# Three tiles find other homes, and the third convolution block's sums run beside its taps, with the conv norm ahead of the later heads' queries and keys

## The chip, the core and the metric

The kernel runs on one core of one Trainium2 chip. The metric is the device time of one execution in microseconds. The engines are TensorE (PE, with its weight loads as PEld), VectorE (DVE), ScalarE (ACT), GpSimd (POOL) and SyncE (SP), which here only issues DMAs.

## The reference

One layer of a hybrid decoder on x of 1024 tokens by 1024 features, all in float32:

```python
h = rms_norm(x, norm1_g)
q, k, v, glu_a, glu_b = split(h @ w_in)          # 5 x 512 columns
A = stick_breaking_attention(norm(q), norm(k), v) # 8 heads x 64, strictly causal
C = swish(layer_norm(causal_depthwise_conv(glu_a * sigmoid(glu_b))))  # width 31, 512 channels
x = x + concat([A, C]) @ w_out
h = rms_norm(x, norm2_g)
g, v = split(h @ w_up)                            # 2 x 2816
x = x + (silu(causal_dwconv3(g)) * v) @ w_down
```

Stick-breaking attention weighs a key by the sigmoid of its score and by the product of one minus the sigmoids of all later keys; the kernel does this with logs, a running sum and an exponential. The layer norm of the convolution is over the 512 channels of a token.

## The kernel before, in words

**Products.** Each float32 operand is split into a high part, rounded to what TensorE takes (`hi`), and a remainder (`lo`). A product is three matmuls: high by high, low by high, high by low (`mm3`, L280 to L283). Products of the queries, keys and values of heads 0 to 3 are 256 columns wide, others up to 512.

**Stages.** The times are those of the profiled execution.
- 0 to 35: the first norm. For each of 8 blocks of 128 tokens (`norm_in`, L383): squares on ScalarE, the root on GpSimd (L273), scaling on VectorE (L393), 8 transposes on TensorE (L402), high part on ScalarE (L406), remainder on VectorE (L407). Value products of heads 0 to 3 stand among the transposes.
- to 134: value and gate products. The convolution works on 4 blocks of 128 channels, numbered 0 to 3 here. It is split into even and odd tokens: the even taps and odd taps on VectorE with their sums in PSUM (`conv_a`, L573 and L575; `conv_b`, L583 and L585), and a third chain on sums of neighbouring inputs (`xs`, made at L559): ScalarE multiplies (L599), GpSimd adds (L602). Three closing sums on VectorE join them (L615, L616, L617; L615 needs the whole third chain).
- 134 to 181: keys and queries of heads 0 to 3. Each result bank is squared by ScalarE (L483), GpSimd takes the root (L272, L273), and ScalarE scales it out of PSUM (L487). Only then is the bank free.
- 181 to 205: values of heads 4 to 7 (copied out at L472).
- 205 to 250: queries and keys of heads 4 to 7 (`qk`) and, among them, the convolution's norm: transposes L638 (`ln`), statistics L642 and L643, scaling L646, transposes back L664 (`lnT`).
- 249 to 456: attention, head after head: keys and queries are transposed (`kT` L922, `qT` L956), scores `z` (L993 to L996), weights on ScalarE (`wt`, L1008), running sums on VectorE (L1023), products on GpSimd (L1026), transposes (`wT`, L1049), a remainder `tl` (L1059), and the output `po` (L1065, L1066). The score chain of a head leaves TensorE waiting unless other products fill it: the rest of `qk` early, and the convolution's half of the out projection (`op`) later.
- 456 to 516: attention's half of the out projection (`opa`), the second norm (L1303, L1311) and the operand blocks for the feed-forward.
- 516 to 939: the up projection, a loop over 22 blocks of features. Block products follow a Strassen-like scheme with 7 products for 8.
- 939 to the end: the down projection (`dn`, L1623). Each result bank is added to up to four sums of the output (`c11`, `c21`, `c12`, `c22`) on VectorE (L1626). The sums begin with x, loaded by DMA. The weights are split at L1531 to L1533.

**The order.** Up to the end of attention the order is not written out: each piece of work is an operation of a `Plan` with an engine, a cost, a key (`T(us)`, the wanted time, in units of 8 us), operations that it comes after, and tokens for rooms in PSUM and SBUF (`"s"` is the three banks for transposes). A list scheduler takes the ready operation that can start first; among those that start within `PATIENCE` (in ns) of an engine's being free, the smaller key wins. The order that comes out is then fixed on PE, DVE, ACT and POOL. SP's queue and all later stages are ordered by the tile scheduler. Rooms in SBUF are reused when the last reader of the old tile is done, so a tile's home decides when a load into it may begin.

Of the kernel before, what the change touches and what calls it, by code (L numbers as in the profile page):

```python
# [31 lines left out]
LEAD_LOAD, LEAD_W = 14.0, 11.0  # L32
LN_AT = 195.0
# [3 lines left out]
HORIZON, PATIENCE = 3.0, 50  # L37
AHEAD_Z, AHEAD_SCAN = 1.7, 0.9
QK_FROM, QK_TO = -3.0, 6.0
CONV_FROM, CONV_TO = 7.0, 31.0  # L40
W_SHIFT = 0.0
# [135 lines left out]
def kernel(  # L177
# [54 lines left out]
    const([P, 24], F32, "pad")  # L232

    ident = const([P, P], F32, "ident")
    make_identity(nc, ident)
    ident_b = const([P, P], BF16, "ident_b")
    nc.vector.tensor_copy(ident_b, ident)
    ident_r = const([P, P], F32R, "ident_r")
    nc.vector.tensor_copy(ident_r, ident)
# [46 lines left out]
    small = ctx.enter_context(tc.tile_pool(name="small", bufs=1))  # L286
    mix_ctx = ExitStack()
    mixp = mix_ctx.enter_context(tc.tile_pool(name="mixp", bufs=1, reuse_waits="tile"))
    attn_out = mixp.tile([P, ND // 2, S], F32, tag="attn_out", name="attn_out")
# [4 lines left out]
    for tag in ("v0", "k0", "q0", "k1", "q1", "v1"):  # L294
        tile_of = qkvp.tile([P, 2, D], F32, tag=tag, name=f"x_{tag}")
        if tag not in ("v0", "k0"):
            xs.append(tile_of)
# [3 lines left out]
    wp = in_ctx.enter_context(tc.tile_pool(name="wp", bufs=1, side="right", reuse_waits="tile"))  # L301
    hp = hp_ctx.enter_context(tc.tile_pool(name="hp", bufs=1, side="right", reuse_waits="tile"))
# [33 lines left out]
    for n in range(2):  # L336
        h_hi.append(hp.tile([P, ND, HS], F32R, tag=f"hh{n}", name=f"h_hi{n}"))
        h_lo.append(hp.tile([P, ND, HS], F32R, tag=f"hl{n}", name=f"h_lo{n}"))
# [9 lines left out]
                 "qd": 2, "squares": 1, "whl": 8, "pair": 2, "norm": 4, "xsum": 2, "cacc": 2, "term": 3, "ln": 4},  # L348
# [93 lines left out]

    def project(part, blk, ws, pairs, ats):

        done.setdefault((part, blk), [])
        for pair, at_ in zip(pairs, ats):
# [31 lines left out]
            def square(d=d, pair=pair, dst=dst, o=o):  # L478
                d["sq"], d["rs"] = [small.tile([P, 8], F32, tag=f"{tag}8_{o.index}", name=f"{tag}_{part}{blk}_{pair}") for tag in ("sq", "rs")]
                d["to"] = dst().rearrange("p t (h d) -> p (t h) d", d=DH)  # L480
                d["from"] = d["ps"].rearrange("p t (h d) -> p (t h) d", d=DH)
                for i in range(8):
                    nc.scalar.activation(d["to"][:, i, :], d["from"][:, i, :], AF.Square, accum_out=d["sq"][:, i:i + 1])  # L483

            def scale(d=d):
                for i in range(8):
                    nc.scalar.activation(d["to"][:, i, :], d["from"][:, i, :], AF.Copy, scale=d["rs"][:, i:i + 1])  # L487

            a = add("ACT", 3500, square, T(at_ + 6), [m])
            b = add("POOL", 2700, lambda d=d: rstd(d["rs"], d["sq"], 1.0 / DH), T(at_ + 6), [a])  # L490
            a = add("ACT", 1850, scale, T(at_ + 6), [b])
            o.users += [a]
            done[part, blk] += [a]
# [21 lines left out]
    def glu(c, ws, ats, conv_at, conv_to):  # L515
# [73 lines left out]
        for m in range(HALF + 1):  # L589
# [11 lines left out]
            x = add("ACT", 720, times, key(m, 16), [summed], [tm])  # L601
            last = add("POOL", 1310, lambda e=e: nc.gpsimd.tensor_tensor(d["c"], d["c"], e["t"], op=ALU.add), key(m, 16), [x, last])  # L602
# [178 lines left out]
    def queries_keys_in(t, at_):  # L781
# [3 lines left out]
        for k in range(ND):  # L785
            def products(k=k):
                if k == 0:
                    d["ps"] = bank(o, [P, 512], f"qk{t}")
                for part in "qk":
# [435 lines left out]
    for name, tag in (("11", "hh0"), ("21", "hl0"), ("22", "hh1"), ("T2", "hl1")):  # L1225
        new_block([name], hp, tag)
# [437 lines left out]
```

## Time and profile before

| | |
|---|---|
| median of 3 runs | 1165.71 us (1164.83 to 1165.88) |
| profiled execution, its own time | 1162.9 us |
| its span | 1161.1 us |
| mean granted clock of TensorE | 0.987 |
| matmuls | 5734 |

A profiled execution's span begins with its first instruction and ends with its last. In windows and groups, busy times are in us; a bracket behind a row of a timeline gives the time that the engine was idle before it and what ended that time. Since TensorE is nearly always busy, what counts is where it isn't, and where its clock is below 1.00.

### The profile page before, as it was taken

The page shows a single profiled execution, that of the slowest core. Times are in us where ns is not written, and L with a number is a line of the kernel's source. Part 1 is how long each engine was busy: PE and PEld are TensorE (multiplying, and loading weights), DVE is VectorE, ACT ScalarE, POOL GpSimd, SP SyncE. Part 2 cuts the span into 40 slices and gives each one's busy share as a digit, 9 for nine tenths or more (in the row PEclk, how much of TensorE's full clock was granted, in tenths as well). Part 3 has the DMA queues.
Part 4 walks back from the last instruction along what each step waited for, and adds up shares of the span by engine and source line. Part 5 has one row for each costly group of instructions (what it writes and reads, how often), then busy time and mean ns, then how long its engine had stood idle before and what let it go on. Part 6 is the DMA issues. An engine that isn't in the chain of part 4 may idle for free.

```text
span 1161.1 us, 16180 instructions
## 1 busy us (share of the span) xinstructions
PE 1118.5 (96%) x5734; PEld 936.9 (81%) x5734; DVE 909.5 (78%) x1199; ACT 640.3 (55%) x1335; POOL 603.2 (52%) x505
## 2 busy tenths in 40 slices
PE   6999999989999997979999999999999989999998
PEld 5888899767788886868888888888888867888886
DVE  5399995549998888889887777777677679887895
ACT  6255576586987885554434333434333466766680
POOL 6077965486666652545522332233313167877880
PEclk8999999999999998989999999999999999999999
DMA  8011103122743114432332222222222461134303
GB/s 276 19 56 55 55 2 91 47 102 95 232 126 110 55 39 153 154 127 65 118 109 71 93 73 91 73 91 73 91 86 79 133 247 70 77 145 146 130 16 145
DMA packets 108638, 116.50 MB, mean 100 GB/s; under 512 B 20782, under 2 KB 88590, under 8 KB 108558
## 3 DMA queue, kind: packets, MB, share of 16 engines
q1 hardware_dynamic: 108414, 114.95, 30.0%
q8 instruction: 45, 0.74, 0.3%
q10 hardware_dynamic: 144, 0.52, 0.1%
q14 instruction: 35, 0.29, 0.1%
HBM read 82.95 MB, written 28.31 MB: 96 GB/s over the span
## 4 chain that ended last, share of the span: by engine, by line
PE 84%; DVE 6%; POOL 4%; ACT 3%; issue 2%; DMA 1%; SPq 0%; POOLq 0%; DVEq 0%; ACTq 0%
PE dn L1623 16%; PE u_S L281 7%; PE u_S L282 7%; PE u_S L283 7%; PE u L282 5%; PE u L281 5%; PE u L283 5%; PE wT L1049 2%; POOL attn_out L602 2%; PE po L1066 2%; PE v L281 1%; PE po L1065 1%; PE v L282 1%; PE v L283 1%; PE z L996 1%
## 5 line engine op out<-in xcount | busy, mean ns | idle before, releaser
L1623 PE MATMUL dn<-wd,wd 128*128 128x512 f32 x924 | 212.4, 390 | 5.3 <-DVE c L1626 2.7
L1623 PEld LDWEIGHTS dn<-wd,wd 128*128 128x128 f32 x924 | 172.6, 188 | 44.9 <-DVE c L1626 4.8
L1626 DVE TENSOR_TENSOR c<-dn,c 128x512 f32<-128x512 f32 x144 | 95.2, 683 | 24.1 <-PE dn L1623 22.8
L602 POOL TENSOR_TENSOR attn_out<-attn_out 128x512 f32<-128x512 f32 x60 | 83.3, 1389 | 54.2 <-ACT attn_out L599 50.4
L1532 ACT CAST wd<-rawd 128x512 fp32r<-128x512 f32 x154 | 87.0, 618 | 42.1 <-PE dn L1623 15.8
L1026 POOL TENSOR_TENSOR wt<-wt,nb 128x128 f32<-128x128 f32 (+3 forms) x64 | 78.2, 1228 | 56.6 <-DVE nb L1023 34.1
L282 PE MATMUL u_S<-bT,aS 128*128 128x512 f32 x264 | 102.7, 389 | 0.0
L283 PE MATMUL u_S<-bT,aS 128*128 128x512 f32 x264 | 102.7, 389 | 0.0
L281 PE MATMUL u_S<-bT,aS 128*128 128x512 f32 x264 | 102.4, 389 | 0.0
L277 ACT CAST aS<-rawu 128x512 fp32r<-128x512 f32 x63 | 39.0, 621 | 94.8 <-PE u_S L283 70.6
L1023 DVE TENSOR_TENSOR_SCAN nb<-nb,one 128x128 f32<-128x128 f32 (+3 forms) x64 | 85.3, 1344 | 6.8 <-ACT nb L1005 6.6
L1533 DVE TENSOR_TENSOR wd<-whole,wd 128x512 fp32r<-128x512 f32 x110 | 73.7, 683 | 10.7 <-ACT wd L1532 8.4
L1392 POOL TENSOR_TENSOR s<-rawu 128x512 f32<-128x512 f32 x21 | 29.9, 1426 | 99.5 <-DMA rawu<-in_w_up_dram 89.3
L1531 ACT COPY whole<-rawd 128x512 f32<-128x512 f32 x110 | 63.0, 584 | 29.7 <-DMA rawd<-in_w_down_dram 15.7
L1398 POOL TENSOR_TENSOR rawu<-rawu 128x512 f32<-128x512 f32 x21 | 29.0, 1381 | 82.3 <-DVE a L278 82.3
L282 PE MATMUL u<-b,a 128*128 128x512 f32 x176 | 70.0, 398 | 0.0
L281 PE MATMUL u<-b,a 128*128 128x512 f32 x176 | 69.9, 397 | 0.0
L283 PE MATMUL u<-b,a 128*128 128x512 f32 x176 | 69.2, 393 | 0.0
L277 ACT CAST a<-rawu 128x512 fp32r<-128x512 f32 x63 | 39.0, 621 | 51.5 <-PE u_S L283 34.7
L1487 DVE SCALAR_TENSOR_TENSOR y<-gv,cols_a,y 128x1023 f32<-128x1023 f32 (+1 forms) x44 | 58.6, 1333 | 8.3 <-ACT y L1485 8.2
L1533 POOL TENSOR_TENSOR wd<-rawd,wd 128x512 fp32r<-128x512 f32 x44 | 57.5, 1324 | 11.6 <-ACT wd L1532 9.7
L278 DVE TENSOR_TENSOR a<-rawu,a 128x512 fp32r<-128x512 f32 x63 | 47.0, 748 | 15.8 <-ACT a L277 15.8
(286 smaller groups left out, 3363.7 us busy)
## 6 DMA issues: line engine op xcount, KB each, us to landing
rawu<-in_w_up_dram SPq DMA_DIRECT2D x44, 512.0 KB
act_d<-y SPq DMA_DIRECT2D x22, 512.0 KB
rawd<-act_d SPq DMA_DIRECT2D x22, 512.0 KB
rawd<-in_w_down_dram SPq DMA_DIRECT2D x22, 512.0 KB
rawo<-in_w_out_dram SPq DMA_DIRECT2D x8, 512.0 KB
m<-conv_d SPq DMA_DIRECT2D x16, 256.0 KB
xt<-in_x_dram SPq DMA_DIRECT2D x8, 512.0 KB
x_part<-xt SPq DMA_DIRECT2D x8, 512.0 KB
```

Of the source, the lines that this page charges most:

```text
L277: nc.scalar.copy(hi, src)
L281: nc.tensor.matmul(ps, a_hi, b_hi, start=first, stop=False)
L282: nc.tensor.matmul(ps, a_hi, b_lo, start=False, stop=False)
L283: nc.tensor.matmul(ps, a_lo, b_hi, start=False, stop=last)
L602: last = add("POOL", 1310, lambda e=e: nc.gpsimd.tensor_tensor(d["c"], d["c"], e["t"], op=ALU.add), key(m, 16), [x, last])
L1023: nc.vector.tensor_tensor_scan(rev, rev, one.to_broadcast([P, w]), 1.0, op0=ALU.mult, op1=ALU.bypass)
L1026: nc.gpsimd.tensor_tensor(d["wt"][:, :w], d["wt"][:, :w], d["nb"][:, o + 1:S + 1], op=ALU.mult)
L1531: nc.scalar.copy(whole, src)
L1532: nc.scalar.copy(t[:, 0], src)
L1533: lo_engine.tensor_tensor(t[:, 1], whole, f32(t[:, 0]), op=ALU.subtract)
L1623: nc.tensor.matmul(ps, a[:, tok], b, start=first and m == 0, stop=last and m == 2, skip_group_check=True)
L1626: nc.vector.tensor_tensor(sums[c][s], ps, sums[c][s], op=ALU.add)
```

## The change

**Three homes.**
- The identity matrix is made in a corner of `attn_out`, and only its rounded copy `ident_r` is kept and read as float32; the room of the old one goes to a small scratch tile.
- `q1` and `k1` (queries and keys of heads 4 to 7) are one tile `qk1`. Queries and keys are normalized by one function, `normalized`: the bank is first copied to SBUF whole (L452 after), and squares (L457) and scaling run from SBUF, so the bank is free after the copy. There are 12 such copies.
- The first half of the high part of h (`hh0`) has a pool of its own (`hp0`). At the end, `c11` and `c21` lie there as one tile `c_1`. Before, they lay over the operand block `T4`, which the last up product reads; now they lie over block `11`, which the first of the last seven products reads. Head 0's keys are split into a tile of the convolution (`first_keys`), and so need not wait until h is free.

**The plan's numbers.**
- The third chain's keys run over 0.6 of the window of a block (`m * 0.6`), and the windows are 29 us, not 33.
- The key of the conv norm (`LN_AT`) is 165, not 195.
- The later token blocks of the first norm are wanted at 10, 12, 14, 16 rather than 20, 23, 26, 29 us of the plan.
- Head 0's keys are wanted 4.0 units ahead of the head's own work (`EARLY`), not 2.6. `PATIENCE` goes from 50 to 200 ns. `LEAD_LOAD` (how far ahead weights are loaded), `QK_TO` (until when the `qk` filler is spread) and `W_SHIFT` (the out projection's weights) change too.

```diff
-LN_AT = 195.0
+LN_AT = 165.0
...
-        norm_in(t, xl[t], (2 + 2 * t) if t < 4 else (8 + 3 * t))
+        norm_in(t, xl[t], (2 + 2 * t) if t < 4 else (10 + 2 * (t - 4)))
...
-    ats = {0: ((24, 35), 47, 80), 1: ((58, 69), 80, 113), 2: ((80, 91), 113, 146), 3: ((102, 113), 146, 179)}
+    ats = {0: ((24, 35), 47, 76), 1: ((58, 69), 76, 105), 2: ((80, 91), 105, 134), 3: ((102, 113), 134, 163)}
...
-            x = add("ACT", 720, times, key(m, 16), [summed], [tm])
+            x = add("ACT", 720, times, key(m * 0.6, 16), [summed], [tm])
...
+    def normalized(name, d, o, m, to, at_):
+        r = plan.token("rs8")
...
+        c = add({"ACT": 600, "DVE": 690}, out_of, T(at_), [m])
+        o.users += [c]
+        a = add("ACT", 3500, square, T(at_), [c], [r])
+        b = add("POOL", 2700, lambda: rstd(d["rs"], d["sq"], 1.0 / DH), T(at_), [a])
+        a = add("ACT", 1850, scale, T(at_), [b])
...
+        k2 = split_op("k", staged, 0, base - (2.6 if h else EARLY), ready, khl)
...
+    sums = hp0.tile([P, 4, D], F32, tag="hh0", name="c_1")
...
-    sums = {c: quarters([dn.tile([P, D], F32, tag=f"c{c}_{k}", name=f"c{c}_{k}") for k in range(2)]) for c in ("11", "21")}
```

**How the order moves.** VectorE, around the second value projection, before. `lo_v` is the remainder of the value weights, `v_1898` the values copied out, `conv_b` the odd taps, and `L615` to `L617` are the closing sums of conv block 3.

```order
90 L585 SCALAR_TENSOR_TENSOR conv_b_1691<-cpad_916,cols_b,conv_b_1691 128x512 x12
91 L433 TENSOR_TENSOR lo_v_0_1810<-raw_v_0_1473,hi_v_0_1809 128x1024
92 L433 TENSOR_TENSOR lo_v_1_1827<-raw_v_1_1475,hi_v_1_1826 128x1024
93 L585 SCALAR_TENSOR_TENSOR conv_b_1691<-cpad_916,cols_b,conv_b_1691 128x512 x2
94 L472 COPY v_1898<-v_2_1899 128x512
95 L472 COPY v_1898<-v_3_1965 128x512
96 L433 TENSOR_TENSOR lo_qk_2070<-raw_qk_1851,hi_qk_2069 128x1024
97 L615 TENSOR_TENSOR attn_out<-attn_out,conv_a_1518 128x512
98 L433 TENSOR_TENSOR lo_qk_2074<-raw_qk_1867,hi_qk_2073 128x1024
99 L616 TENSOR_TENSOR conv_out_2053<-conv_a_1518,conv_out_2053 128x512
100 L617 TENSOR_TENSOR conv_out_2053<-attn_out,conv_b_1691 128x512
```

The same place after. `q_1587` are the queries of heads 0 to 3, with one copy (L452) for each pair of token blocks; L629 to L631 are the closing sums.

```order
88 L599 SCALAR_TENSOR_TENSOR conv_b_1633<-cpad_1112,cols_b,conv_b_1633 128x512 x7
89 L452 COPY q_1587<-q_1_1662 128x512
90 L599 SCALAR_TENSOR_TENSOR conv_b_1633<-cpad_1112,cols_b,conv_b_1633 128x512 x4
91 L452 COPY q_1587<-q_2_1735 128x512
92 L629 TENSOR_TENSOR attn_out<-attn_out,conv_a_1438 128x512
93 L452 COPY q_1587<-q_3_1813 128x512
94 L437 TENSOR_TENSOR lo_v_0_1891<-raw_v_0_1396,hi_v_0_1890 128x1024
95 L437 TENSOR_TENSOR lo_v_1_1895<-raw_v_1_1420,hi_v_1_1894 128x1024
96 L630 TENSOR_TENSOR conv_out_1926<-conv_a_1438,conv_out_1926 128x512
97 L631 TENSOR_TENSOR conv_out_1926<-attn_out,conv_b_1633 128x512
98 L656 BN_STATS st_0_1978<-ln_0_1968 128x6
```

The closing sums moved ahead of the values' copies, and the two value remainders moved from the middle of the taps to behind the first closing sum and the last query copy. TensorE's second matmul of this projection reads `lo_v_0`, directly behind the last query product. On GpSimd, the two remainders of the query weights (on VectorE before) and the input sum of block 2 now stand among the sums of L602 (L616 after).

TensorE, where attention begins, before: `qk` are queries and keys of heads 4 to 7, `lnT` the conv norm's transposes, `z` the scores of head 0.

```order
1378 L922 MATMUL kT_0_2599<-ident_r,keys 128x128 x4
1379 L922 MATMUL kT_1_2604<-ident_r,keys 128x128 x4
1380 L664 MATMUL lnT_2_2610<-ident,attn_out 128x128 x4
1381 L281 MATMUL qk_2561<-hi_qk_2155,h_hi_170 128x512
1382 L282 MATMUL qk_2561<-lo_qk_2156,h_hi_170 128x512
1383 L283 MATMUL qk_2561<-hi_qk_2155,h_lo_171 128x512
1384 L664 MATMUL lnT_3_2630<-ident,attn_out 128x128 x4
1385 L993 MATMUL z_0_0_2635<-keys 128x256
```

The same place after; 15 matmuls of `qk_2570` follow the transposes, and then `z_0_0` stands in row 1358.

```order
1338 L289 MATMUL qk_2515<-hi_qk_2295,h_lo_175 128x512
1339 L939 MATMUL kT_0_2540<-ident_r,first_keys 128x128 x4
1340 L939 MATMUL kT_1_2545<-ident_r,first_keys 128x128 x4
1341 L973 MATMUL qT_0_2550<-ident_r,attn_out 128x128 x4
1342 L973 MATMUL qT_1_2561<-ident_r,attn_out 128x128 x4
1343 L287 MATMUL qk_2570<-hi_qk_2073,h_hi_172 128x512
```

All of the conv norm is now ahead of this place: its transposes stand among the value products and the first `qk` products. Behind the first scores 81 matmuls of `qk` are left, and 57 before. At the end of attention, the last 68 matmuls before `opa` held no other work before; now 12 matmuls of the out projection (3, 6 and 3) stand among them.

VectorE, where the down projection begins, before: `wd` are weight remainders, `gv` and `y` belong to the last up block, `c_0` is the sum `c11`.

```order
805 L1484 TENSOR_TENSOR gv<-u_22_8508,gv 128x512
806 L1533 TENSOR_TENSOR wd_8616<-whole_8617,wd_8616 128x512
807 L1487 SCALAR_TENSOR_TENSOR y_8422<-gv,cols_a,y_8422 128x1022
808 L1533 TENSOR_TENSOR wd_8644<-whole_8645,wd_8644 128x512
809 L1626 TENSOR_TENSOR c_0_8592<-dn_2_0_8624,c_0_8592 128x512
810 L1626 TENSOR_TENSOR c_0_8592<-dn_2_1_8629,c_0_8592 128x512
```

The same place after:

```order
810 L1501 TENSOR_TENSOR gv<-u_22_8520,gv 128x512
811 L1645 TENSOR_TENSOR c_8556<-dn_2_0_8633,c_8556 128x512
812 L1550 TENSOR_TENSOR wd_8625<-whole_8626,wd_8625 128x512
813 L1504 SCALAR_TENSOR_TENSOR y_8434<-gv,cols_a,y_8434 128x1022
814 L1645 TENSOR_TENSOR c_8556<-dn_2_1_8638,c_8556 128x512
815 L1550 TENSOR_TENSOR wd_8653<-whole_8654,wd_8653 128x512
```

The first add of a result bank moved ahead of two weight remainders and one step of `y`, and stands directly behind the last `gv`.

More of the change, by code (lines that the diff above doesn't have):

```diff
@@ L476, in project @@
                 continue
[L478 to L493, printed above, removed]
+            done[part, blk].append(normalized(f"{part}{blk}_{pair}", d, o, m, lambda dst=dst: dst().rearrange("p t c -> p (t c)"), at_ + 6))
     HALF = (KC - 1) // 2
```

124 lines of the change are left out of this document (70 added, 54 removed).

## The prediction

> **What bounds the kernel now.** I read the page first: the busy shares, then the chain that ended last.
>
> ```profile
> PE 1118.5 (96%) x5734; PEld 936.9 (81%) x5734; DVE 909.5 (78%) x1199; ACT 640.3 (55%) x1335; POOL 603.2 (52%) x505
> ...
> PE 84%; DVE 6%; POOL 4%; ACT 3%; issue 2%; DMA 1%; SPq 0%; POOLq 0%; DVEq 0%; ACTq 0%
> ```
>
> TensorE is 96% busy and carries 84% of the chain. The order of both kernels holds the same products, 5734 matmuls, so the change can win only TensorE's idle time and its slow clock. Next I cut the span into stages; the columns are window, length, busy time of PE, PEld, DVE, ACT and POOL with their counts, the granted clock, DMA share and GB/s.
>
> ```profile
> 0.00:40.00 40.00, 30.76 (x194) 25.85 (x195) 21.97 (x28) 22.71 (x39) 17.69 (x27) 0.91 0.60 200
> 120.00:180.00 60.00, 59.56 (x441) 56.95 (x440) 56.52 (x74) 42.89 (x193) 43.04 (x35) 1.00 0.09 27
> 180.00:205.00 25.00, 24.22 (x201) 24.01 (x200) 9.56 (x12) 12.85 (x44) 14.15 (x12) 1.00 0.38 106
> 205.00:240.00 35.00, 33.28 (x172) 26.57 (x172) 18.99 (x33) 19.01 (x80) 19.42 (x28) 1.00 0.20 71
> 240.00:280.00 40.00, 34.60 (x199) 27.35 (x197) 26.99 (x36) 32.34 (x90) 31.53 (x34) 0.96 0.22 71
> 280.00:320.00 40.00, 37.55 (x254) 32.27 (x252) 37.40 (x45) 34.02 (x71) 25.75 (x23) 1.00 0.70 215
> 320.00:440.00 120.00, 118.47 (x793) 101.55 (x792) 106.57 (x126) 96.47 (x205) 75.78 (x63) 1.00 0.27 83
> 440.00:460.00 20.00, 14.37 (x75) 11.93 (x76) 16.78 (x18) 9.40 (x17) 5.00 (x3) 0.83 0.54 184
> ...
> 480.00:520.00 40.00, 34.10 (x148) 26.80 (x147) 34.49 (x44) 23.89 (x45) 23.05 (x22) 0.88 0.44 145
> 520.00:935.00 415.00, 415.00 (x1830) 342.76 (x1829) 315.05 (x382) 161.32 (x235) 139.68 (x96) 1.00 0.28 90
> 935.00:975.00 40.00, 34.71 (x143) 25.57 (x142) 36.38 (x58) 25.63 (x47) 27.67 (x21) 1.00 0.39 145
> ```
>
> The up projection (520 to 935) is solid TensorE; nothing can be won there, and it prices a 512-wide product: 415.00 / 1830 = 0.227 us. The losses lie at the start (9.2 us idle of 40), where attention begins (205 to 320: 1.7 + 5.4 + 2.5 = 9.6 idle, and 0.04 of 40 = 1.6 lost to the clock), at the end of attention (5.6 of 20, clock 0.83), at the second norm (480 to 520) and where the down projection begins (5.3 of 40). Last the waits of TensorE, each with total, times and longest:
>
> ```profile
> PE hT L402 <- DVE x_q L393: 7.6, 2, 4.5
> ...
> PE z L993 <- ACT wt L1008: 5.6, 5, 2.9
> PE po L1066 <- DVE tl L1059: 2.8, 2, 2.5
> PE dn L1623 <- DVE c L1626: 2.7, 4, 1.6
> ...
> PE qk L281 <- ACT k L808: 1.0, 1, 1.0
> PE v L281 <- DVE v L472: 0.8, 1, 0.8
> PE k L281 <- ACT k L487: 0.4, 1, 0.4
> ```
>
> **The change part by part.**
>
> *Start.* Transposes of token blocks 2 to 7 now stand between groups of 12 products, some 50 products earlier than before for the later blocks. Each block needs one scaling and two remainders on VectorE:
>
> ```profile
> L407 DVE TENSOR_TENSOR h_lo<-hT,h_hi 128x512 fp32r<-128x512 f32 x14 | 9.1, 684 | 5.6 <-ACT h_hi L406 5.6
> L393 DVE SCALAR_TENSOR_TENSOR x_q<-x_q,rs,attn_out 128x1024 f32<-128x1024 f32 x4 | 5.1, 1277 | 3.2 <-POOL rs L273 3.2
> ```
>
> ```profile
> 19.81 0.60 PE L402 MATMUL hT<-ident,x_k 128*128 128x128 f32 x4
> 20.16 0.36 PE L281 MATMUL v<-hi_v,h_hi 128*128 128x256 f32 x1
> ```
>
> That is 1.28 + 2 x 0.68 = 2.64 us a block, against 12 products of 256 columns at 0.12 each (180.87 less 180.75, below), 1.44 us, and two groups of four transposes at 0.35 (20.16 less 19.81): 2.1 us. VectorE falls 0.5 us behind per block, 3.0 over the six; a weight remainder that moves off it to GpSimd gives some back. I take +2.0, ends 0 and +3.5. The identity's new home costs nothing: it is made before the first x arrives.
>
> *Projection banks.* Queries and keys are copied out of PSUM whole, and squares, root and scaling run from SBUF. The three bank waits above (0.4, 0.8, 1.0) go: -2.2, ends -2.5 and -0.6. The price is 12 copies of about 0.69 us (the row of the value copy, below) on VectorE or ScalarE, which are both short of full until 280; covered.
>
> *Second value projection.* Here the change adds a wait. Rows of VectorE, with the idle time before and its releaser in brackets, and one of TensorE:
>
> ```profile
> 177.61 4.06 DVE L433 TENSOR_TENSOR lo_v<-raw_v,hi_v 128x1024 fp32r<-128x1024 f32 x2
> ...
> 186.70 0.69 DVE L472 COPY v<-v 128x512 f32<-128x512 f32 x1 [3.58 <-PE v L283]
> ...
> 195.88 0.68 DVE L615 TENSOR_TENSOR attn_out<-attn_out,conv_a 128x512 f32<-128x512 f32 x1
> ...
> 206.11 1.23 DVE L433 TENSOR_TENSOR lo_qk<-raw_qk,hi_qk 128x1024 fp32r<-128x1024 f32 x1 [0.22 <-ACT hi_qk L429]
> ```
>
> ```profile
> 180.75 0.28 PE L281 MATMUL v<-hi_v,h_hi 128*128 128x256 f32 x1
> 180.87 0.28 PE L282 MATMUL v<-lo_v,h_hi 128*128 128x256 f32 x1
> ```
>
> Before, both remainders of the value weights were made at 177.61, ahead of TensorE's need at 180.75. Now, in VectorE's order, they stand behind the conv's first closing sum (which waits for GpSimd's sum chain) and behind the copy of the last query block (which waits for TensorE's last query product). So TensorE ends its queries, at about 182 with the start's delay, and then waits 0.69 for the copy and 1.23 to 2.07 (half of 4.06) for the first remainder: 1.9 to 2.8, with about 0.5 for the hand-overs. I take 3.0, from the idle row 1.23 to the busy one. Behind these queue the other remainder and the conv's last two sums; TensorE has 36 products x 0.12 = 4.3 us before it needs the latter.
>
> A gap of that length may cost clock as well:
>
> ```profile
> 260.25 0.51 PE L993 MATMUL z<-keys 128*128 128x512 f32 x1 [2.95 <-ACT wt L1008]
> ...
> 945.04 1.66 PE L1623 MATMUL dn<-wd,wd 128*128 128x512 f32 x6 [1.59 <-DVE c L1626]
> ```
>
> ```profile
> 260.00:280.00 20.00, 18.13 (x107) 15.02 (x107) 18.79 (x26) 13.79 (x32) 13.94 (x15) 0.91 0.20 66
> ```
>
> After a wait of 2.95 the clock over the next 20 us was 0.91, so 0.09 x 20 = 1.8 us were lost; after one of 1.59 it was 1.00. Between the two I take half, +0.9, ends 0 and 1.8. The Trainium skill (TensorE: Matmul & The Clock Gate, Part 1) has the clock fall only after an idle window of about 3.4 us. By that rule alone this term would be 0 and the sum 0.9 lower; the 2.95 row speaks against it, since a shorter gap cost the clock here.
>
> *Conv norm and the beginning of attention.* The conv's norm (L638, L664) now runs between the value products, not between the queries and keys, and head 0's keys are split ahead of their turn. The first scores stand 27 rows earlier, and 81 products of the queries' and keys' filler are left behind them, against 57: 24 more x 0.227 = 5.4 us of work that can fill the waits for weights, logs and sums at 240 to 280 (5.4 idle, 1.6 of clock: 7.0). The small norm waits at 205 to 240 (1.7 idle) shift to where VectorE is 38% busy (9.56 of 25). I take 5.4 of filled idle and the 1.6 of clock, and leave 0.5 for new ones: -6.5. Ends: -10 (nearly all of 9.6 + 1.6), and -2 (filler that only moves the waits to 280 to 320, where VectorE is 37.40 of 40 busy).
>
> *Steady attention.* 0, ends -1.5 and +1.5: 1.5 us idle in 120, and the same work.
>
> *End of attention.* Before, the last 68 rows hold no filler; now 12 products of the out projection stand among them, 12 x 0.227 = 2.7 us. The places:
>
> ```profile
> 444.48 0.35 PE L1065 MATMUL po<-rest 128*128 128x256 f32 x1 [1.46 <-ACT m L1267]
> 447.29 0.58 PE L1066 MATMUL po<-tl,rest 128*128 128x256 f32 x1 [2.45 <-DVE tl L1059]
> ```
>
> They cover at most their own 2.7 us and with luck the clock (0.17 x 20 = 3.4). I take -2, ends -4 and 0.
>
> *Second norm.* Same work; loads of x and weights change places in SyncE's queue. 0, ends -2 and +2.
>
> *Start of the down projection.* Two of the output sums now lie over a block that is read by the first of the last seven products, not by the last, so their loads come early, and the add that frees the first bank stands ahead of two weight remainders.
>
> ```profile
> 944.29 1.37 DVE L1626 TENSOR_TENSOR c<-dn,c 128x512 f32<-128x512 f32 x2 [1.05 <-DMA c<-x_d]
> ```
>
> The 1.05 goes; some of TensorE's 2.7 us on these adds goes with it, but VectorE stays near full (36.38 of 40) and only swaps what is late. I take -1.5, ends -4 and 0.
>
> Sum: +2.0 - 2.2 + 3.0 + 0.9 - 6.5 - 2.0 - 1.5 = -6.3. The profiled execution took 1162.9 us (span 1161.1), so 1156.6; the median of the runs is 1165.71, 2.8 above the profiled one, so 1159.4.
>
> **The rivals.**
>
> *A. The third sum chain ends late (slower).* Rows of GpSimd:
>
> ```profile
> 118.69 21.43 POOL L602 TENSOR_TENSOR attn_out<-attn_out 128x512 f32<-128x512 f32 x15
> ...
> 140.08 2.31 POOL L559 TENSOR_TENSOR attn_out<-cpad 128x527 f32<-128x527 f32 x1
> ...
> 189.44 5.44 POOL L602 TENSOR_TENSOR attn_out<-attn_out 128x512 f32<-128x512 f32 x4
> ```
>
> ```profile
> L433 POOL TENSOR_TENSOR lo_k<-raw_k,hi_k 128x1024 fp32r<-128x1024 f32 x1 | 2.9, 2879 | 0.0
> ```
>
> The chain ended at 194.88. GpSimd was busy 43.04 from 120 to 180 and 14.15 after; the change adds two query remainders (2 x 2.88) and one input sum (2.31): 65.3 us, so without any idle it ends at 185; TensorE's products of block 2 end 96 wide and 384 narrow products ahead of 180.75 (21.8 + 46.1 us), at 112.9, so after its input sum (2.31) the chain of block 2 can begin at about 115.2, not at 118.69, which takes 3.5 off: 182. For the rival: that needs a GpSimd that hardly idles, and it idled 17 of those 60 us. Against it: VectorE's taps end by about 177.5 (186.70 less its idle 3.58 is 183.1 before; less the 4.06 that moved behind and some for the moved query remainders), and ScalarE was 42.89 of 60 busy, so it can feed the chain. If the chain ends where it did, the first remainder is there at 194.9 + 0.68 + 0.69 + 1.23 = 197.5, and TensorE waits 15.5 rather than 3.0: +12.5, and the whole 1.8 of clock: -6.3 + 12.5 + 0.9 = +7.1, 1173. It decides from a chain end of 181.3 + 6.3 = 187.6 on. Chance 0.17.
>
> *B. Attention paces itself (no change).* If the early scores only wait for VectorE (106.57 of 120 busy further on), the 6.5 of the beginning and the 2 of the end don't come: -6.3 + 8.5 = +2.2, 1167.9. Against it: VectorE has room at 240 to 280 (26.99 of 40), where the waits lie. Chance 0.13, of which 0.11 within the bound.
>
> *C. All hidden gains come.* Start 0, beginning -10, end -4, down -4: 0 - 2.2 + 3.9 - 10 - 4 - 4 = -16.3, 1149.4. Chance 0.14.
>
> **How the numbers follow.** The forecast has 0.56, with an own range of 1152 to 1163. What a measurement can tell from no change is 0.2%, 2.3 us. Faster: 0.56 + 0.14 = 0.70; same 0.11; slower 0.17 + 0.02 = 0.19. The range of 8 in 10 leaves out the far half of C and of A: 1151 to 1170.
>
> **What would show it.** Right: first scores about 3 us earlier than before (+2.0 - 2.2 + 3.9, less 5.4 for the 24 products behind them and the 1.7 idle at 205 to 240), a wait of about 3 us on the value remainder near 182, no wait of over 1.5 us on weights between 240 and 280, clock 1.00 there, less than 4 idle at 440 to 460, and no DMA ahead of the first down adds. Wrong: a wait of over 9 us at the second value products (A), attention's end no earlier against the opening of the out projection although the scores began early (B), or a start that costs over 4 us.

## The result, and the profile after

The changed kernel is slower: 1182.18 us median of 4 runs (1180.72 to 1183.64), against 1165.27 of 4 runs of the kernel before. The ratio is 1.0146, with a 95% interval of 1.0128 to 1.0163. The forecast was 1159.4, with a range of 1151 to 1170. Its sign was wrong, and its range did not hold the time. The profiled execution took 1180.72, with a span of 1178.9 (17.8 more than before).

The page's totals and chain of the changed kernel:

```profile
PE 1128.0 (96%) x5734; PEld 943.5 (80%) x5734; DVE 915.6 (78%) x1208; ACT 652.9 (55%) x1324; POOL 618.0 (52%) x518
...
PE 76%; DVE 8%; ACT 7%; POOL 4%; DMA 3%; issue 2%; SPq 0%; DVEq 0%; POOLq 0%; ACTq 0%
```

TensorE has the same 5734 matmuls, but carries 76% of the chain rather than 84%. VectorE, ScalarE and DMA took the rest: the chain now leaves TensorE more often. The stages (same columns as before):

```profile
0.00:40.00 40.00, 29.07 (x179) 23.78 (x180) 24.67 (x29) 23.59 (x40) 18.37 (x28) 0.87 0.61 200
120.00:180.00 60.00, 60.00 (x430) 56.84 (x429) 56.51 (x80) 45.91 (x152) 53.49 (x44) 1.00 0.12 36
180.00:205.00 25.00, 20.21 (x151) 19.81 (x150) 13.97 (x22) 19.96 (x81) 14.24 (x19) 0.86 0.25 69
205.00:240.00 35.00, 34.63 (x221) 30.77 (x221) 15.30 (x23) 25.30 (x72) 18.23 (x21) 1.00 0.25 87
240.00:280.00 40.00, 36.17 (x193) 28.90 (x192) 23.74 (x31) 30.81 (x98) 24.20 (x28) 0.96 0.26 79
280.00:320.00 40.00, 37.01 (x246) 30.19 (x244) 38.86 (x51) 31.66 (x67) 27.45 (x25) 1.00 0.54 163
```

Up to 40 and from 180 to 205 TensorE lost more than before (idle 10.9 and 4.8, with clocks of 0.87 and 0.86). From 205 to 280 it lost less (idle 4.2 against 7.1). The waits of TensorE:

```profile
PE h2T L1328 <- DVE h L1320: 9.7, 4, 4.9
PE hT L406 <- DVE x_q L397: 6.3, 2, 3.7
PE hT L406 <- DVE x_qk L397: 3.0, 2, 1.5
PE dn L1642 <- DVE c L1645: 3.0, 2, 2.1
PE opa L288 <- DVE loo L1219: 2.9, 1, 2.9
PE v L287 <- ACT hi_v L433: 2.9, 1, 2.9
...
PE z L1010 <- ACT wt L1025: 1.9, 4, 0.8
PE v L288 <- DVE lo_v L437: 1.9, 1, 1.9
```

New are the scaling of `x_qk` (3.0), the out projection's remainder `loo` (2.9), and both parts of the value weights (2.9 and 1.9). The second norm's wait grew from 5.9 to 9.7. The waits for attention weights fell from 5.6 to 1.9, as was forecast.

**A ledger of the loss.** TensorE does the same matmuls in nearly the same order, so its lag can be read anywhere: the start of a matmul less the sum of the issue times of all matmuls ahead of it (0.227 us for 512 columns, 0.12 for 256, 0.11 for a transpose). The points are rows of its order, and the times are those of the profiled executions. "Mended a" and "homes only" are kernels of the experiments below.

| point (row) | before | changed | mended a | homes only |
|---|---|---|---|---|
| keys begin (627) | 13.0 | 17.9 | 12.8 | 12.8 |
| second value products (1107) | 14.5 | 25.1 | 13.8 | 13.2 |
| 300 to 310 us (1700) | 32.0 | 36.0 | 24.1 | 34.8 |
| 320 to 330 us (1800) | 32.3 | 41.0 | 30.4 | 35.3 |
| near attention's end (2594) | 40.6 | 52.5 | 38.0 | 43.4 |
| out projection opens (2651) | 49.3 | 58.1 | 47.2 | 52.1 |
| within it (2739) | 49.4 | 63.0 | 47.2 | 52.1 |
| second norm done (2900) | 61.4 | 80.2 | 57.9 | 63.0 |
| down begins (4707) | 62.5 | 80.1 | 58.4 | 63.5 |
| 93 products later (4800) | 70.6 | 88.0 | 66.2 | 70.7 |

Each difference between two rows is one stage. Changed less before: start +4.9; keys, queries and second values +5.7; conv norm and early attention -6.6; the next 100 products +4.7; attention +0.1 in two parts (+3.2, then -3.1); opening of the out projection +4.8; second norm +5.2; up -1.2; down -0.2. That is 17.4 of the 17.8. The issue times are rough, so a single step is good to about half a us: read from the trace, the first key product, with the same 658 matmuls ahead of it, starts at 133.98 before and at 138.34 after, so the start lost 4.4 rather than 4.9.

**The start.** VectorE and GpSimd of the changed kernel:

```profile
23.54 3.01 DVE L397 SCALAR_TENSOR_TENSOR x_qk<-x_qk,rs,attn_out 128x1024 f32<-128x1024 f32 x1
...
27.67 3.01 DVE L397 SCALAR_TENSOR_TENSOR x_qk<-x_qk,rs,attn_out 128x1024 f32<-128x1024 f32 x1
```

```profile
23.08 2.40 POOL L437 TENSOR_TENSOR lo_glu_b<-raw_glu_b,hi_glu_b 128x1024 fp32r<-128x1024 f32 x1
...
27.20 2.40 POOL L437 TENSOR_TENSOR lo_glu_a<-raw_glu_a,hi_glu_a 128x1024 fp32r<-128x1024 f32 x1
```

Two scalings took 3.01 us where one alone takes 1.28. Both began within 0.5 us after GpSimd had begun a weight remainder, and both ended about 1.07 us after its end (26.55 after 25.48, 30.68 after 29.60), nearly as long as a scaling takes by itself. The transposes behind them waited 1.45 and 1.53 us.

**The second value products.** ScalarE, VectorE, GpSimd and TensorE:

```profile
186.38 1.98 ACT L433 CAST hi_v<-raw_v 128x1024 fp32r<-128x1024 f32 x2
```

```profile
184.68 0.69 DVE L629 TENSOR_TENSOR attn_out<-attn_out,conv_a 128x512 f32<-128x512 f32 x1 [4.04 <-POOL attn_out L616]
185.28 0.68 DVE L452 COPY q<-q 128x512 f32<-128x512 f32 x1
187.44 3.39 DVE L437 TENSOR_TENSOR lo_v<-raw_v,hi_v 128x1024 fp32r<-128x1024 f32 x2 [1.48 <-ACT hi_v L433]
```

```profile
180.60 4.04 POOL L616 TENSOR_TENSOR attn_out<-attn_out 128x512 f32<-128x512 f32 x3
```

```profile
184.29 0.28 PE L289 MATMUL q<-hi_q,h_lo 128*128 128x256 f32 x1
187.46 0.38 PE L287 MATMUL v<-hi_v,h_hi 128*128 128x256 f32 x1 [2.89 <-ACT hi_v L433]
189.75 0.58 PE L288 MATMUL v<-lo_v,h_hi 128*128 128x256 f32 x1 [1.91 <-DVE lo_v L437]
190.13 0.41 PE L289 MATMUL v<-hi_v,h_lo 128*128 128x256 f32 x1
190.34 0.41 PE L287 MATMUL v<-hi_v,h_hi 128*128 128x256 f32 x1
```

The conv's sum chain ended at 180.60 + 4.04 = 184.64, as TensorE's queries did: rival A's point of 187.6 wasn't reached. VectorE did wait 4.04 us for it, though, and had the closing sum and the last query copy behind it only by 185.96. The rounded copy of the value weights (`hi_v`) was later still: ScalarE began it at 186.38, behind query squares and scalings. The remainder followed at 187.44, 1.48 us after VectorE was free, and after the two waits the products ran at half clock (0.41 us long, and 0.21 apart rather than 0.12, until 194.6).

```profile
160.00:190.00 30.00, 25.21 (x207) 24.81 (x207) 23.85 (x33) 29.12 (x118) 26.63 (x24) 0.96 0.01 2
```

In these 30 us ScalarE was 29.12 busy and GpSimd 26.63. The same window before:

```profile
160.00:190.00 30.00, 29.22 (x244) 29.01 (x243) 23.03 (x28) 23.36 (x118) 20.31 (x17) 1.00 0.12 36
```

### The profile page after: what moved, and what is told of

Read it like the earlier page. It is cut to its first block, busy times and chain, and to the rows that moved or that the text cites. A ratio compares the mean times of both kernels' runs of the same rounds, so it can differ in the third digit from the quotient of the medians.

```text
span 1178.9 us, 16183 instructions
## 1 busy us (share of the span) xinstructions
PE 1128.0 (96%) x5734; PEld 943.5 (80%) x5734; DVE 915.6 (78%) x1208; ACT 652.9 (55%) x1324; POOL 618.0 (52%) x518
## 4 chain that ended last, share of the span: by engine, by line
PE 76%; DVE 8%; ACT 7%; POOL 4%; DMA 3%; issue 2%; SPq 0%; DVEq 0%; POOLq 0%; ACTq 0%
PE dn L1642 16%; PE u_S L288 7%; PE u_S L289 7%; PE u_S L287 7%; PE u L288 5%; PE u L289 5%; PE u L287 5%; POOL attn_out L616 3%; PE wT L1066 2%; ACT junk L457 2%; DVE nb L1040 1%; PE po L1083 1%; PE z L1013 1%; PE v L288 1%; PE v L289 1%
## 5 line engine op out<-in xcount | busy, mean ns | idle before, releaser
L1549 ACT CAST wd<-rawd 128x512 fp32r<-128x512 f32 x154 | 87.4, 618 | 37.1 <-DMA rawd<-act_d 13.2
L616 POOL TENSOR_TENSOR attn_out<-attn_out 128x512 f32<-128x512 f32 x60 | 80.7, 1345 | 7.2 <-ACT attn_out L613 3.2
L1550 POOL TENSOR_TENSOR wd<-rawd,wd 128x512 fp32r<-128x512 f32 x44 | 57.9, 1333 | 12.8 <-ACT wd L1549 12.0
L1076 DVE TENSOR_TENSOR tl<-wT,rest 128x512 fp32r<-128x512 f32 x80 | 53.5, 682 | 8.1 <-ACT rest L1070 6.9
```

Of the source, the lines that this page charges most:

```text
L1549: nc.scalar.copy(t[:, 0], src)
L1550: lo_engine.tensor_tensor(t[:, 1], whole, f32(t[:, 0]), op=ALU.subtract)
```

## The experiments

All times are medians. The ratio is to the kernel before on the same chips. That of the changed kernel is 1.0146 (1.0128 to 1.0163).

**1. The gate weights' remainders later.** They keep to GpSimd and are planned behind the last scaling of the first norm.

```diff
+    [(glu0[part]["ready"].after.append(scaled[-1]), glu0[part]["ready"].cost.pop("DVE")) for part in "ba"]
     project("v", 0, v0, (0, 1), (12, 18))
```

> The changed kernel, but the two first gate-weight remainders stay on GpSimd and wait until the last scaling of the first norm is done. Theory (two engines in each other's way): the scalings of blocks 4 and 5, which took 3.01 us beside these remainders, take about 1.3 again, TensorE's waits of 1.45 and 1.53 us for them go, and the time falls from 1182.2 by 3 to 4, to about 1178.5. Rival (VectorE's row of work per block is itself too long at the start): the scalings get shorter, but the waits move elsewhere in the start, and the time falls by under 1.5.

Measured: 1178.50, ratio 1.0114 (1.0098 to 1.0129), 3.7 less. VectorE's and GpSimd's rows:

```profile
25.79 1.27 DVE L397 SCALAR_TENSOR_TENSOR x_qk<-x_qk,rs,attn_out 128x1024 f32<-128x1024 f32 x1
...
30.58 3.00 DVE L397 SCALAR_TENSOR_TENSOR x_v<-x_v,rs,attn_out 128x1024 f32<-128x1024 f32 x1
```

```profile
30.11 2.39 POOL L437 TENSOR_TENSOR lo_glu_b<-raw_glu_b,hi_glu_b 128x1024 fp32r<-128x1024 f32 x1
```

The two slow scalings are back at 1.27. The plan's order let GpSimd begin a remainder at 30.11, just ahead of the last scaling, and now that one takes 3.00: the slow operation goes where the remainder goes. The theory holds for the scalings. How much of the 3.7 is theirs is less sure: in the profiled executions the first key product came 1.9 earlier (136.45, before the edit 138.34), and the spans differ by the same 1.9. The Trainium skill (SBUF — State Buffer, Who interferes with whom) says that a VectorE instruction with two inputs in SBUF contends with a GpSimd instruction that reads SBUF. The trace agrees: 3.01 against 1.28. The taps of the convolution, which take their running sum from PSUM, ran beside GpSimd's sums in the kernel before and took the same 0.755 throughout (0.742 to 0.757):

```profile
L585 DVE SCALAR_TENSOR_TENSOR conv_b<-cpad,cols_b,conv_b 128x512 f32<-128x512 f32 x42 | 31.7, 755 | 1.4
```

**2. The value weights' rounded copy earlier.**

```diff
-        a = add("ACT", 1060, high, T(at_ - LEAD_W), [x], d["rooms"])
+        a = add("ACT", 1060, high, T(at_ - LEAD_W if hi_at is None else hi_at), [x], d["rooms"])
```

Here `hi_at` is `at_ - 22` for the second value weights, and None for all others.

> The changed kernel, but the rounded copy of the second value weights is wanted 11 us earlier by ScalarE, so that it and its remainder stand ahead of the last query work. Theory (the loss at the second value products is ScalarE's and VectorE's queue, not the conv's sum chain): the waits of 2.89 and 1.91 us and the slow clock behind them go, about 1.5 us come back as a wait for the conv's closing sums, and the time falls by 4 to 6, to about 1177. Rival (the conv's sum chain rules here): TensorE then waits as long for the conv's sums at the norm's transposes, and the time falls by under 2.

Measured: 1172.88, ratio 1.0066 (1.0044 to 1.0088), 9.3 less, more than expected. TensorE's rows at the same place:

```profile
184.22 0.28 PE L289 MATMUL q<-hi_q,h_lo 128*128 128x256 f32 x1
184.34 0.28 PE L287 MATMUL v<-hi_v,h_hi 128*128 128x256 f32 x1
184.46 0.28 PE L288 MATMUL v<-lo_v,h_hi 128*128 128x256 f32 x1
```

No wait and no slow clock are left; the ledger's lag at row 1107 falls from 25.1 to 17.2. The wait that I had expected in its place did not come, because more value products stand ahead of the norm's transposes in this order (48 rather than 36). The cause was the place of the weights' two steps in the queues. The edit does not part these two, for it moved the remainder too: on VectorE its first half now begins at 177.44, among the taps and ahead of the closing sum. So ScalarE's lateness is shown only for the 1.48 us that VectorE waited for it in the changed kernel. With the rounded copy in time, the remainder behind the sum chain and the query copy would have begun at 185.96, and TensorE would still have waited some 3 us (an estimate from the rows above: half of 3.39 is 1.7, so 187.7, and the queries end at 184.4).

**3. The homes alone.** All numbers of the plan are as before; the homes and the copies out of PSUM stay.

> The changed kernel with all numbers of the plan as before (start times, windows, chain keys, norm key, patience, lead of loads, filler end, weight shift, head 0's lead); only the three homes and the copies out of PSUM are left. Theory (the plan's numbers brought the losses): 1160 to 1166, no slower than before. Rival (the copies and the squares from SBUF load ScalarE and VectorE, and that is the loss): over 1170.

Measured: 1164.26, ratio 0.9991 (0.9980 to 1.0002): no difference that can be told. The copies cost nothing that shows, and the numbers brought the loss.

**4. One transfer moved.** The store of the last partial sum of x stands ahead of the load of the first up weights.

```diff
             nc.sync.dma_start(d[n], w_up_k[:, :, n * DFF:n * DFF + P])
+            tc.add_manual_dep(nc.cur_bb.bb.instructions[-1], stored[NT - 1].name, mybir.DependencyInfo(
+                mybir.DependencyClass.NoSync, mybir.DependencyReason.DATA), reason="queue order")
```

`stored[NT - 1]` is the last store of a partial sum of x; the line sets an order in the queue and no wait.

> The changed kernel with one transfer moved: the store of the last partial sum of x stands ahead of the load of the first up weights in SyncE's queue, as before the change; nothing else differs. Theory: the 2.60 us that VectorE waited for that store before the last remainder of the out projection's weights goes, TensorE's wait of 2.90 in the out projection shrinks to under 1, and the time falls by 2.5 to 4. Rival (the remainder is late for other reasons): under 1.

Measured: 1179.93, ratio 1.0126 (1.0111 to 1.0141), 2.3 less, a little under the expectation. TensorE's wait in the out projection:

```profile
469.96 0.50 PE L288 MATMUL opa<-loo,m 128*128 128x512 f32 x1 [0.76 <-DVE loo L1219]
```

It was 2.90 at this place. In the changed kernel the load waited for its room until 462.85, and the store behind it (463.32) held the room of the last weight remainder: a queue's order, as the theory said. VectorE's row there in the changed kernel:

```profile
469.01 1.23 DVE L1219 TENSOR_TENSOR loo<-rawo,hio 128x1024 fp32r<-128x1024 f32 x1 [2.60 <-DMA x_part<-xt]
```

The intervals of the two kernels overlap, so the 2.3 itself is uncertain.

**5. The weight shift back.**

```diff
-W_SHIFT = 0.5
+W_SHIFT = 0.0
```

> The changed kernel with the shift of the out projection's weights back to 0. Theory: the three late remainders of these weights, for which TensorE waited 2.0 us where the out projection's filler begins and lost 4.5 us against the same row before, are ready in time: the time falls from 1182.2 by 3 to 4.5, to about 1178.5. Rival (VectorE is full there whichever way the weights stand, 38.86 of 40 at 280 to 320): the wait moves to attention's own remainders, under 1.5.

Measured: 1179.78, ratio 1.0128 (1.0109 to 1.0147). TensorE no longer waits for these remainders, but at the first product for the sum of attention's output:

```profile
315.62 0.80 PE L287 MATMUL op<-w_hh,m 128*128 128x512 f32 x1 [1.79 <-DVE attn_out L1107]
```

In the ledger the step from row 1700 to 1800 is 6.6, against 5.0 in the changed kernel. So the wait moved, as the rival said. The median is 2.4 lower, which this stage does not explain, and the intervals overlap.

**6. The out projection's remainders earlier.**

```diff
-            w_attn[k][1], d["raw"], f32(w_attn[k][0]), op=ALU.subtract), key, [a])
+            w_attn[k][1], d["raw"], f32(w_attn[k][0]), op=ALU.subtract), key - 1.0, [a])
```

> The changed kernel with the remainders of the weights for the attention half of the out projection wanted 8 us earlier by VectorE, so the first stands five rows earlier, ahead of some of the last head's work. Theory: with them the rooms of the next two weights come free earlier, the waits at the opening of this projection (2.90 us and the slow clock, 4.8 in all) go mostly, and the time falls by 2.5 to 5. Rival (attention's end is paced by the last head's running sums, which now wait for the remainders): under 1, or slower.

Measured: 1177.71, ratio 1.0106 (1.0082 to 1.0131), 4.5 less. The lag grows by 1.7 from row 2651 to 2739 (57.7 to 59.4), and by 4.9 in the changed kernel. The theory holds, though the four runs spread over 5.7 us.

**7. The sums' home alone, on the kernel before.**

> The kernel before with only the new home of two of the output sums (over the block that the first of the last products reads); nothing else differs up to the down projection. Theory (my term for the down projection, 1.5, was too large, since VectorE is full there): within 1 us of the kernel before, 1164.5 to 1166. Rival (the term holds): 1163 to 1164.

Measured: 1165.52, ratio 1.0000 (0.9991 to 1.0010). The term of 1.5 for the down projection was nothing. In the changed kernel the early loads did what they should, and the loss came 12 us later:

```profile
956.30 10.20 PE L1642 MATMUL dn<-wd,wd 128*128 128x512 f32 x42
968.62 1.83 PE L1642 MATMUL dn<-wd,wd 128*128 128x512 f32 x5 [2.12 <-DVE c L1645]
```

TensorE now runs 42 products without a wait, and before 18; then it waits 2.12 for the same adds.

**8. Edits 1, 2, 4, 5 and 6 together.**

> The changed kernel with the edits of the first, second, fourth, fifth and sixth experiment together. Theory (five local waits, each to be had back by itself, no pacing elsewhere): 1182.2 less 3.7, 9.3, about 4 and about 4 is 1161, and so 1159 to 1164, faster than before by a little. Rival (they overlap, or attention paces itself): 1166 to 1172.

Measured: 1171.56, ratio 1.0060 (1.0042 to 1.0079). The expectation of 1159 to 1164 failed. The lag at row 2739 is 52.2, near the 49.4 of before, but from there to row 2900 it grows by 18.4 (before 12.0): the second norm, which none of the edits touched, keeps its loss.

**9. The patience of the second plan back.**

```diff
-                rank = (max(start - PATIENCE, at[e]), op.key) if op.key <= main[low].key + 1 else (start, op.key)
+                rank = (max(start - self.patience, at[e]), op.key) if op.key <= main[low].key + 1 else (start, op.key)
```

`self.patience` is 200 in the first plan and 50 in the second.

> The changed kernel, but the second plan (out projection of attention, second norm, first operands) is made with the patience of before, 50 ns; the first plan keeps 200. Theory (the longer patience also reordered VectorE there, and this is why all kernels with the changed numbers lose some 5 us more than before between 480 and 550): TensorE's waits for the second norm fall from 9.7 to about 6 us, and the time falls from 1182.2 by 4 to 6. Rival (that stage loses because data from attention's end come late): waits and time as they were, within 1.5.

Measured: 1176.58, ratio 1.0099 (1.0077 to 1.0121), 5.6 less. The wait for the second norm:

```profile
PE h2T L1328 <- DVE h L1320: 5.7, 4, 2.0
```

In the changed kernel its longest case was this, on VectorE and TensorE:

```profile
525.09 3.44 DVE L1341 TENSOR_TENSOR bT<-t,bT 128x512 fp32r<-128x512 f32 x2
528.46 1.75 DVE L1341 TENSOR_TENSOR bT<-raws,bT 128x512 fp32r<-128x512 f32 x1
530.12 1.39 DVE L1320 SCALAR_TENSOR_TENSOR h<-x,rs,g 128x512 f32<-128x512 f32 x2
```

```profile
531.00 1.94 PE L1328 MATMUL h2T<-ident_r,h 128*128 128x128 f32 x8 [4.85 <-DVE h L1320]
```

Operand remainders that could wait stood ahead of the scaling that TensorE waited for.

**10. The patience of before in both plans.**

```diff
-HORIZON, PATIENCE = 3.0, 200
+HORIZON, PATIENCE = 3.0, 50
```

> The changed kernel with the patience of before, 50 ns, in both plans; all else as changed. In its order the value remainders stand ahead of the conv's first closing sum, and the last partial sum of x is stored ahead of the up weights. Theory (one number brought most of the losses behind 180): the stage around the second norm gives back 5, the opening of the out projection 4 to 5, the second value products 2 to 4; the start keeps its 4.9: 1182.2 falls to 1168 to 1172. Rival (each loss came with another number, patience only with the second norm): 1176 to 1178.

Measured: 1166.52, ratio 1.0018 (1.0009 to 1.0027), 15.7 less, even below the range of the theory. This one number took back most of the 16.9. By the ledger the opening of the out projection has no loss left (52.9 at row 2651, 52.8 at 2739), the second norm loses 11.9 as before, and the start 1.5 more than before rather than 4.9. The value weights still cost 6.2 from row 819 to 1107. A patience of 200 on the kernel before, without the other changes, was not run, so it isn't shown that the number costs as much by itself.

**11. Mended a.** Patience 50, the start times of before, and edits 2 and 4; homes, windows, chain keys, norm key, head 0's lead and the other numbers stay.

> The changed kernel with patience 50 in both plans, the start times of before, the second value weights' rounded copy 11 us earlier, and the store of x ahead of the up weights. Kept are the homes, the conv's windows and chain keys, the norm's key, head 0's lead, the lead of loads and the filler's end. Theory: start 4.9, value products 7.4, second norm 5, opening of the out projection 4 and steady attention up to 3 come back: 1158 to 1162, faster than the kernel before by 0.3 to 0.6%. Rival (what the earlier norm and scores gain is given back in steady attention): 1163 to 1167.

Measured: 1161.27, ratio 0.9968 (0.9958 to 0.9978). It beats both kernels by a small but clear amount.

**12. Mended b.** As mended a, but with a patience of 200 in the first plan and edit 6.

> As the kernel run before it, but the first plan keeps the patience of 200, and the out projection's remainders are wanted 8 us earlier. Theory (patience in the first plan costs some 3 us in steady attention): 2 to 4 slower than that kernel. Rival (steady attention loses for another reason, such as where the filler's products lie): within 1 of it.

Measured: 1162.69, ratio 0.9985 (0.9975 to 0.9994): 1.4 slower, between the two expectations, and the intervals overlap. Its lag grows by 13.0 from row 1800 to 2594 and by 4.5 to row 2651; in mended a by 7.6 and 9.3. The sums are 17.5 and 16.9 (before 17.0, changed 17.2). That fits products that are kept for attention's end, cover that end, and are missing earlier. Two numbers differ between these kernels, so the 1.4 can't be put down to one of them.

**13. Two of the out projection's remainders on GpSimd.** On mended a.

```diff
-        b = add("DVE", 1300, lambda: nc.vector.tensor_tensor(
+        b = add("POOL" if k in (1, 3) else "DVE", 2450 if k in (1, 3) else 1300, lambda: (nc.gpsimd if k in (1, 3) else nc.vector).tensor_tensor(
             w_conv[k][1], wd[k], f32(w_conv[k][0]), op=ALU.subtract), C0 + W_SHIFT + 0.1 * k, [a])
```

> The mended kernel a, with two of the four remainders of the out projection's first weights made on GpSimd rather than VectorE. Theory (what the early scores gained is given back at about 300 to 320 because these four remainders, 5.8 us, fall on a VectorE that is full there): VectorE's row of three, 4.59 us, becomes one of about 1.5 to 3, TensorE gives back 2 to 4 us less between rows 1700 and 1800 of its order, and the time falls from 1161.3 to 1158 to 1160. Rival (the give-back comes from the lack of filler while the weights come in, whoever makes the remainders; GpSimd takes 2.4 to 2.9 for each): within 1 of mended a, or slower.

Measured: 1161.28, ratio 0.9964 (0.9952 to 0.9976), the same as mended a. VectorE's row of three remainders is gone, but the lag still grows by 5.6 from row 1700 to 1800 (6.3 in mended a). GpSimd now has this:

```profile
304.60 5.72 POOL L1134 TENSOR_TENSOR w_hl<-rawo,w_hh 128x1024 fp32r<-128x1024 f32 x2
```

VectorE's remainders alone are not the cause. Either all helpers are full there, or the filler is missing: the weights' room comes free only when the last `qk` product is done. This stays open.

**14. What the title names, alone.** Homes, windows, chain keys and the norm's key; all other numbers as before.

> The changed kernel with only what the change's title names: the homes, the conv's windows and chain keys, and the norm's key; start times, patience, lead of loads, filler's end, weight shift and head 0's lead as before. In its order the value remainders stand just ahead of the conv's first closing sum. Theory (the ideas of the title are worth a little, and the other numbers cost): a wait of 2 to 4 at the second value products, the norm's gain kept in part: 1160 to 1165. Rival (the title's own numbers cost at the value products more than they bring): 1166 to 1169.

Measured: 1165.20, ratio 0.9998 (0.9989 to 1.0006). The title's ideas cost at the second value products (the lag goes from 13.4 at row 915 to 20.7 at row 1107), and bring about the same again behind them, part in early attention and the rest up to the second norm. TensorE's waits at the value products:

```profile
182.13 0.38 PE L287 MATMUL v<-hi_v,h_hi 128*128 128x256 f32 x1 [1.37 <-ACT hi_v L433]
185.61 0.58 PE L288 MATMUL v<-lo_v,h_hi 128*128 128x256 f32 x1 [3.10 <-DVE lo_v L437]
```

Here the remainder stands ahead of the closing sum, so the sum chain has no part in these waits. The rounded copy began at 181.05, and VectorE came to the remainder only at 184.34, behind five taps. The order on both engines makes the wait, whatever the weights' steps stand behind.

## Why the prediction was wrong, step by step

The sum said -6.3 and the ledger says +17.4, 23.7 apart. Two stages that the sum put at nothing, the opening of the out projection and the second norm, make 10.0 of this. The second value products were under-priced by about 4 together with the banks, early attention's gain was counted without the 4.7 lost right behind it, and the start was under-priced by 2 to 3.

- **Start, +2.0: measured 4.4 to 4.9**, over the 4 that the prediction had named as a sign of being wrong. The step took 1.28 for every scaling. But the gate weights' remainders on GpSimd, one of them newly moved there and counted as a relief for VectorE, made two scalings 3.01 (shown by experiment 1). Rows of before held the sign of it, a scaling of 1.97 that began beside such a remainder:

```profile
19.76 1.97 DVE L393 SCALAR_TENSOR_TENSOR x_k<-x_k,rs,attn_out 128x1024 f32<-128x1024 f32 x1
```

```profile
17.62 3.03 POOL L433 TENSOR_TENSOR lo_glu_b<-raw_glu_b,hi_glu_b 128x1024 fp32r<-128x1024 f32 x1
```

- **Banks, -2.2: about -0.9.** The three waits went, and a new one of 1.3 came, for the copy of a `qk` bank.
- **Second value products, +3.9: about +7.4 against the queries' end.** The wait that the step described was there: sum chain, copy, remainder, some 3 us of it. But the step followed VectorE alone. It did not ask when ScalarE would make the rounded copy that the remainder needs, and it called the copies out of PSUM "covered" with ScalarE "short of full until 280", from windows in which its load was still that of before. ScalarE was full (29.12 of 30), and the waits came to 4.80. The half clock after them, priced at 0.9, came whole: 21 products 0.21 rather than 0.12 apart, about 2. Experiment 2 had all of it back.
- **Conv norm and beginning of attention, -6.5: measured -6.6 by row 1700.** The mechanism was right: the waits for weights fell from 5.6 to 1.9. That the size fits so well is partly luck. The traces have 81 and 54 products of `qk` behind the first score, so 27 moved (6.1 us), not 24. And the 1.6 of clock, counted as won, was lost again (0.96 from 240 to 280), behind two new waits with four transposes between them:

```profile
247.38 0.66 PE L973 MATMUL qT<-ident_r,attn_out 128*128 128x128 f32 x4 [1.33 <-ACT keys L943]
249.34 0.79 PE L287 MATMUL qk<-hi_qk,h_hi 128*128 128x512 f32 x1 [1.30 <-DVE qk L452]
249.93 0.63 PE L288 MATMUL qk<-lo_qk,h_hi 128*128 128x512 f32 x1
250.36 0.63 PE L289 MATMUL qk<-hi_qk,h_lo 128*128 128x512 f32 x1
```

  The first scores, forecast about 3 us earlier than before, came 5.2 later (254.39 and 249.19), for what had been lost ahead of them was more than the products moved behind them. Last, the step ended at 280 us. In the next 100 products 4.7 were given back, and in mended a 6.3. The prediction had set this end of the range at -2 ("filler that only moves the waits to 280 to 320"), and that is where the sum belonged. Who gives it back is open (experiments 5 and 13).
- **End of attention, -2: measured -3.1, and +3.2 ahead of it.** The 12 products cover the end, but they are the filler of steady attention, priced at 0. A filler that is moved has a price where it stood.
- **Opening of the out projection: not priced, +4.8.** The order had shown that the load of the up weights went ahead of the store of x, and the prediction passed over it with "loads of x and weights change places in SyncE's queue. 0". Experiments 4 and 6 show two causes, that queue (2.3) and the late remainders (4.5); together they are more than the stage lost, so they overlap.
- **Second norm, 0 with ends of 2: measured +5.2.** "Same work" was true, but the longer patience also reordered this plan on VectorE, and the prediction took its order for unchanged. Experiment 9 shows it.
- **Down projection, -1.5: -0.2.** The transfer was early, and VectorE was late instead, as the step had feared.
- **Rival A** had the right place, but not the event: the sum chain ended at 184.6, nearer the 182 worked out for it than the 187.6 where the rival begins, and ScalarE's queue added to the wait. **Rival B** was right in part: the gain was paid back, though not in steady attention.

The failure as a whole was one of method. The sum followed the named ideas of the change, and took the numbers beside them for detail. Putting one of these back, the patience of the scheduler, took off 15.7 of the 16.9 us.

## What to carry to other kernels

When a scheduler's number changes, compare the whole order on every engine, stage by stage, and price each place where a step that TensorE waits for went behind one that it doesn't; a tie-break 150 ns longer cost more here, beside the other changes, than all the named moves together. For a product that waits on a weight, follow every engine that makes that weight, the rounded copy and the remainder, and the queue that loads it. A gain at one point counts only when it is still there at the end of the stage: a lag per row of TensorE's order shows at once which stage keeps it and which gives it back.

## What the hardware showed that was not expected

- VectorE's scaling with two inputs in SBUF took 3.01 us rather than 1.28 when it began within 0.5 us after a GpSimd remainder, and 1.97 when it began 2.1 us after; in all four cases shown it ended 1.07 to 1.08 us after the remainder's end. The conv's taps, with one input in PSUM, took 0.76 in either case.
- After two waits of 2.89 and 1.91 us, with one matmul between them, TensorE's products ran at half clock for 4.5 us (from 190.1 to 194.6). The mean clock of 0.86 from 180 to 205 amounts to 7 us at half, so part of it fell into the waits. Two waits of 1.33 and 1.30 with four transposes between them were followed by half clock too (products of 512 columns 0.43 apart, mean clock 0.96 from 240 to 280), though a single one of 1.59 before the change was not.
